# An encoder layer with Fourier and attention head groups: layout changes by transposing DMAs instead of TensorE transposes, for queries, keys and the input of the output projection

## The chip, the cores and the metric

The kernel runs on one core of a Trainium2 chip. The metric is the device time of one execution in microseconds (us). The engines are TensorE (PE: matrix products and transposes; its weight loads are listed apart as PEld), VectorE (DVE), ScalarE (ACT), GpSimd (POOL) and SyncE (SP, which here does nothing but issue DMAs). Each runs its own instructions in the order in which they were written and waits for the others through semaphores.

## The reference

One layer: RMS norm, an input projection, two head groups side by side, an output projection, a residual add and a final RMS norm. All data are float32.

```python
SEQ, N_META, D_MODEL, HEAD_DIM = 4096, 16, 1024, 64   # 8 query heads, 2 key/value heads
h = concat([meta_tokens, x])                          # 4112 tokens
u = rmsnorm(h, norm_g)
f_in, f_gate, q, k, v, a_gate = split(u @ w_in)       # widths 512, 512, 512, 128, 128, 512

# Fourier group: 8 groups of 64 channels, real part of a 2-D DFT over (tokens, channels)
fr = real(fftn(f_in.reshape(L, 8, 64), axes=(tokens, channels), norm="ortho"))
f_out = (einsum("lgc,gcd->lgd", fr, w_fmix) + b_fmix) * silu(f_gate)

# attention group
q, k = apply_rope(rmsnorm(q, q_g)), apply_rope(rmsnorm(k, k_g))
a_out = softmax(q @ k.T * 64 ** -0.5) @ v * silu(a_gate)

h = h + concat([f_out, a_out]) @ w_out
out = rmsnorm(h, final_g)[N_META:]
```

## The kernel before

**Number format.** A product of precision near float32 is made of f16 pieces: each operand is split into a high half, its f16 rounding, and a low half, the f16 rounding of the rest. The product is then hi x hi + lo x hi + hi x lo, summed in PSUM. So the tiles that feed TensorE exist as a pair of f16 tiles.

**First part, the projections** (`phase_a`). 33 token tiles of 128 tokens (the last holds the 16 meta tokens) go through the kernel one behind the other. For each tile, TensorE makes keys and values (`tile_kv`), queries (`tile_q`) and the two gates (`tile_gate`); `tile_norm` normalises and rotates queries and keys; `tile_stack` splits them into halves, with one head's high and low half side by side in 128 columns (`qs`, `ks`); and `tile_tr`, one tile later, brings them into the layout in which the attention contracts them, with the 128 columns on the partitions. It does this with four TensorE transposes for the keys (L389) and eight for the queries (L396), into PSUM tiles `kt` and `qt` of a pool with two buffers, which the small product `pr` of the row scales shares. DVE copies `kt` out and ACT copies `qt` out, and DMAs store both to DRAM (`k_d`, `q_d`, one block per tile, already transposed). A hand-made plan deals pieces of the Fourier group's fold and projection (`fold_...`, `fproj`) into four slots of each tile.

**Second part, attention and output** (`phase_b`). Keys lie in SBUF, one tile per kv head (`K0`, loaded in the first part at a point of the plan, and `K1`). Queries of a block of 512 tokens are loaded three times: as `qA` (high and low half on 128 partitions), `qB` (the high half, with rows for the score maximum below it) and `qP` (the high half of two heads above each other, for the search of the maximum). The loop runs over 32 pairs: 8 blocks of 512 tokens by 4 pairs of heads. A pair has 66 steps, 33 key tiles for each of two heads. A step makes the scores of one key tile (L1108, L1109, PSUM `s` with two buffers), an exponential on ACT (L1112), a rounding remainder on POOL or DVE (L1114), and, five steps later, the products with V (L1129 to L1136). Between the steps stand the search of the next pair's maximum (`max_units`, L1040 and the reduction L1041 on DVE) and the output projection of the block before, one 128-token tile per pair. At step 12 `out_tr` transposes the tile with eight f32 TensorE transposes (L1172), four from the mixed half `mf` and four from the attention half `obs`; ACT makes the high half `mh` and DVE the low half `ml`; the 48 products of `out_units` follow at steps 15 to 38 and 39 to 62. The last block has no following pair; its output projection is the tail, with `tail_tr` for the transposes (L1354).

**The Fourier group's end.** Its inverse (17 DFT units; `f_step`) is worked through in two stretches. Seven units stand in the initial stage, between the search groups of the first pair's maximum, and have `early` set; ten stand in the first block's attention (`block0`). A unit is: 26 or 50 products (`dft_units`, PSUM `pd`), the `gather` by three ACT instructions into `stk` (L870, L872, L873), four transposes in `trans` (L895), their split into `thl` (L897, L898 on ACT, L901 on DVE, L902 on POOL), and `mix`: products with the mixing weights (L88), the result into `mo` (on ACT, L949, and the bias on POOL, L954, for early units; on DVE, L951, for the others) and on POOL the product with the gate (L956). The rows of `mo` are then held for a DMA to `mf_d` (f32, 512 columns), which `release` issues from the SP queue when the next unit is gathered. `mo` has two buffers.

**Queues.** All loads and stores of the second part are issued by SP in the order of the program; the stores of queries and gates in the first part go through ACT's queue (`adma`).

Of the kernel before, what the change touches and what calls it, by code (L numbers as in the profile page):

```python
# [22 lines left out]
F32 = mybir.dt.float32  # L23
# [9 lines left out]
P = 128  # L33
D = 1024
# [20 lines left out]
def emit(tc, a):  # L55
# [4 lines left out]
    with top:  # L60
# [7 lines left out]
        q_d = dr.tile([NT, P, NH, P], F16, name="q_d")  # L68
        k_d = dr.tile([NT + 1, P, 4, P], F16, name="k_d")
# [3 lines left out]
        mf_d = dr.tile([NTOK, 512], F32, name="mf_d")  # L73
# [56 lines left out]
def phase_a(tc, a, pool, mm3, id16, id32, sc):  # L130
# [16 lines left out]
    with ExitStack() as st:  # L147
# [4 lines left out]
        pp = pool(st, "pp", 4, PSUM)  # L152
        pt = pool(st, "pt", 2, PSUM)
# [12 lines left out]
        ksb = [wp.tile([P, 2, 2, 2, HD], F16, name=f"ks{i}") for i in range(2)]  # L166
# [205 lines left out]
        def tile_stack(t):  # L372

            n, qn, ks = xs[t][0], live[t]["t1"], ksb[pos[t] % 2]
# [9 lines left out]
        def tile_tr(t):  # L384
            n, ks = xs.pop(t)[0], ksb[pos[t] % 2]
            z = live.pop(t)
            kt = pt.tile([P, 8, P], F16, tag="pt", name="kt")
            for i in range(4):
                T.transpose(kt[:, i, :n], ks[:n, i // 2, i % 2].rearrange("p a b->p (a b)"), id16[:n, :n])  # L389
            ko = w2.tile([P, 4, P], F16, tag="ko", name="ko")  # L390
            V.tensor_copy(ko[:, :, :n], kt[:, 0:4, :n])
            store(k_d[t, :, :, :n], ko[:, :, :n])
            if t < NT:
                qt = pt.tile([P, 8, P], F16, tag="pt", name="qt")
                for h in range(NH):
                    T.transpose(qt[:, (h % 2) * 4 + h // 2], z["qs"][:, h].rearrange("p a b->p (a b)"), id16)  # L396
# [353 lines left out]
def phase_b(tc, a, pool, mm3, id32, id16, sc):  # L750
# [6 lines left out]
    dma = nc.sync.dma_start  # L757
# [3 lines left out]
    with ExitStack() as st:  # L761
# [9 lines left out]
        K = [ld["kk"][0], bp.tile([P, NT + 1, 2, P], F16, name="K1")]  # L771
        VV = bp.tile([P, NT + 1, 2, 129], F16, name="VV")
        qA = [bp.tile([P, 4, NH, P], F16, name=f"qA{i}") for i in range(2)]
        qB = [bp.tile([P, 4, NH, P], F16, name=f"qB{i}") for i in range(2)]
        qP = [bp.tile([P, 4, 4, P], F16, name=f"qP{i}") for i in range(2)]
        nm = [bp.tile([P, P], F16, name=f"nm{i}") for i in range(2)]
        G.memset(K[1][:, NT, :, NMETA:], 0.0)
# [7 lines left out]
        def qload(b, part=(0, 1)):  # L785
            src = q_d[4 * b:4 * b + 4].rearrange("t p h c->p t h c")
            if 0 in part:
                for e in range(2):
                    dma(qP[b % 2][64 * e:64 * e + 64], src[0:64, :, 4 * e:4 * e + 4])
# [26 lines left out]
        bias, stk8 = (w2.tile([P, 512], F32, tag="mf", name=n) for n in ("bias", "stk8"))  # L816
# [117 lines left out]
        def mix(u, early):  # L934
# [21 lines left out]
            G.tensor_tensor(out=mo[:n], in0=mo[:n], in1=fgs.pop(u)[:n], op=ALU.mult)  # L956
# [605 lines left out]
```

## Time and profile before

| | us |
|---|---|
| median of three runs | 3243.61 |
| the three runs | 3244.94, 3240.65, 3243.61 |
| span of the profiled execution | 3240.9 |

| engine | busy us in the profiled execution | share of the span | instructions |
|---|---|---|---|
| PE | 3189.1 | 98% | 32919 |
| DVE | 2375.5 | 73% | 3246 |
| ACT | 1703.2 | 53% | 2969 |
| POOL | 2264.4 | 70% | 2172 |

The span reaches from the first to the last instruction of the one execution that the hardware profiler recorded; the runs are timed by themselves, and the profiled execution has its own time, 3240.9 us, just above the fastest of the three. The page gives shares of the whole span. The span consists of stages with different limits, so a share says little about any one of them; the views by stretch and the list of waits say more. In the chain of work that ended last, TensorE has 91% of the span, and the largest single rows are the scores and the products with V.

### The profile page before, as it was taken

The numbers are of one execution on the slowest core, as the hardware profiler recorded it, in microseconds if no ns is written. First come the engines' busy times: TensorE is split into PE (matmuls) and PEld (weight loads), VectorE is DVE, ScalarE is ACT, GpSimd is POOL, SyncE is SP. The second block draws the span as 40 slices with busy tenths as digits, with TensorE's granted clock in tenths as the row PEclk, the third lists the DMA queues.
The fourth block names the chain that finished last, engine by engine and source line by source line (L and its number), as shares of the span: only waits on it lengthen the run. The fifth ranks groups of instructions, "written<-read, shape, count | busy, mean of one in ns | idle before, by whom it ended". The sixth has DMA issues, their size and how long they took to land.

```text
span 3240.9 us, 78233 instructions
## 1 busy us (share of the span) xinstructions
PE 3189.1 (98%) x32919; PEld 1879.4 (58%) x32919; DVE 2375.5 (73%) x3246; ACT 1703.2 (53%) x2969; POOL 2264.4 (70%) x2172
## 2 busy tenths in 40 slices
PE   8999999998999999999999999999999999999998
PEld 4665555555666655555555555555555555555564
DVE  7656566647677777777777778777777877778764
ACT  5443433434555555555555555555555555555553
POOL 4655455536777778777777777777787777777762
PEclk9999999999999999999999999999999999999999
DMA  7443344638322210002001000100110020000011
GB/s 249 134 160 138 136 154 145 198 140 250 118 78 85 77 50 21 21 21 63 21 21 47 21 21 24 47 21 21 33 52 21 21 47 21 25 21 21 21 37 59
DMA packets 139572, 232.00 MB, mean 72 GB/s; under 512 B 22131, under 2 KB 78275, under 8 KB 136275
## 3 DMA queue, kind: packets, MB, share of 16 engines
q1 hardware_dynamic: 125394, 201.83, 19.8%
q10 hardware_dynamic: 13824, 25.17, 2.1%
q8 instruction: 257, 4.21, 0.5%
q14 instruction: 97, 0.79, 0.1%
HBM read 160.58 MB, written 66.38 MB: 70 GB/s over the span
## 4 chain that ended last, share of the span: by engine, by line
PE 91%; DVE 4%; issue 2%; DMA 1%; ACT 1%; POOL 1%; SPq 0%; ACTq 0%; POOLq 0%; DVEq 0%
PE s L1109 14%; PE s L1108 14%; PE o L1129 13%; PE po L1189 9%; PE m L1040 8%; PE o L1136 8%; PE ps L303 5%; PE ps L304 5%; PE ps L306 4%; PE o L1134 2%; PE o L1132 2%; PE pd L857 2%; PE m L1369 1%; PE m L1172 1%; PE pf L86 1%
## 5 line engine op out<-in xcount | busy, mean ns | idle before, releaser
L1114 POOL TENSOR_TENSOR rr<-pe 128x512 f16<-128x512 f32 x1572 | 1680.3, 1085 | 523.4 <-ACT pe L1112 517.9
L1112 ACT ACTIVATE pe<-s 128x512 f32<-128x512 f32 x2112 | 1260.3, 597 | 1031.8 <-PE s L1109 880.6
L1041 DVE TENSOR_REDUCE mx<-m 128x2 f32<-128x1024 f32 x1024 | 1205.7, 1219 | 174.7 <-PE m L1040 169.3
L1136 PE MATMUL o<-VV,rr 128*128 128x65 f16 x8448 | 975.9, 193 | 0.0
L1136 PEld LDWEIGHTS <-rr 128*128 128x128 f16 x8448 | 785.5, 98 | 168.8 <-POOL rr L1114 1.5
L1129 PE MATMUL o<-VV,pe 128*128 128x129 f16 x6336 | 841.0, 222 | 0.5 <-ACT tt L1140 0.4
L1109 PE MATMUL s<-qB,K 128*128 128x512 f16 x2112 | 800.6, 379 | 1.4 <-DVE qB L1076 1.4
L1129 PEld LDWEIGHTS <-pe 128*128 128x128 bf16 x6336 | 591.2, 98 | 362.1 <-issue 191.3
L1108 PE MATMUL s<-qA,K 128*128 128x512 f16 x2112 | 799.8, 379 | 0.7 <-ACT pe L1112 0.7
L1114 DVE TENSOR_TENSOR rr<-pe 128x512 f16<-128x512 f32 x540 | 450.5, 835 | 230.3 <-ACT pe L1112 225.9
L1132 PE MATMUL o<-VV,pe 128*128 128x65 f16 x2112 | 411.5, 195 | 0.0
L1134 PE MATMUL o<-VV,pe 128*128 128x64 f16 x2112 | 410.7, 194 | 0.0
L303 PE MATMUL ps<-wh,xh 128*128 128x512 f16 (+2 forms) x1032 | 353.3, 354 | 8.0 <-ACT xh L291 8.0
L304 PE MATMUL ps<-wl,xh 128*128 128x512 f16 (+2 forms) x1032 | 353.1, 354 | 2.7 <-DVE wl L274 2.7
L1040 PE MATMUL m<-K,qP 64*128 64x512 f16 x2048 | 313.2, 382 | 6.5 <-DMA qP<-q_d 2.4
L306 PE MATMUL ps<-wh,xl 128*128 128x512 f16 x768 | 292.1, 380 | 0.0
L1134 PEld LDWEIGHTS <-pe 128*128 128x128 bf16 x2112 | 209.2, 99 | 0.0
L1132 PEld LDWEIGHTS <-pe 128*128 128x128 bf16 x2112 | 206.6, 98 | 0.0
L1109 PEld LDWEIGHTS <-K 128*128 128x128 f16 x2112 | 205.2, 97 | 1.7 <-issue 1.6
L1108 PEld LDWEIGHTS <-K 128*128 128x128 f16 x2112 | 203.5, 96 | 0.9 <-issue 0.4
L1040 PEld LDWEIGHTS <-qP 64*128 64x128 f16 x2048 | 59.9, 94 | 226.5 <-issue 224.0
L1189 PE MATMUL po<-woh,mh 128*128 128x512 f16 x448 | 169.8, 379 | 0.9 <-DVE hh L1194 0.9
(213 smaller groups left out, 3561.1 us busy)
## 6 DMA issues: line engine op xcount, KB each, us to landing
room<-x SPq DMA_DIRECT2D x32, 512.0 KB
xt<-xt SPq DMA_DIRECT2D x32, 512.0 KB
sg<-fx SPq DMA_DIRECT2D x16, 1024.0 KB
xr<-x SPq DMA_DIRECT2D x32, 512.0 KB
out<-yo SPq DMA_DIRECT2D x32, 512.0 KB
ct<-cdo SPq DMA_DIRECT2D x9, 1088.0 KB
fg_d<-g ACTq DMA_DIRECT2D x32, 256.0 KB
ag_d<-g ACTq DMA_DIRECT2D x32, 256.0 KB
```

What stands on the lines that cost most here:

```text
L303: T.matmul(o, xh[:, d, :n], wh[:, d, c0:c1], start=d == 0, stop=False)
L304: T.matmul(o, xh[:, d, :n], wl[:, d, c0:c1], start=False, stop=False)
L1040: T.matmul(t[:, e], q[rs, s, p], K[kv][rs, 4 * c:4 * c + 4, 0], start=True, stop=True)
L1041: V.tensor_reduce(mx[:, s, :, c], t, axis=AX.X, op=ALU.max)
L1108: T.matmul(s, K[kv][:, t, 0], qa, start=True, stop=False)
L1109: T.matmul(s, K[kv][:, t, 1], qb, start=False, stop=True)
L1112: S.activation(pe, s, AF.Exp, scale=HD ** -0.5)
L1114: eng.tensor_tensor(out=rr, in0=pe, in1=hi, op=ALU.subtract)
L1129: T.matmul(o[:, c0:c0 + 129], hi[:, cs], va, start=t == 0 and s == 0, stop=t == NT, skip_group_check=True)
L1132: T.matmul(o[:, c0:c0 + 65], hi[:, cs], vh, start=False, stop=t == NT, skip_group_check=True)
L1134: T.matmul(o[:, c0:c0 + 64], hi[:, cs], vl, start=False, stop=t == NT, skip_group_check=True)
L1136: T.matmul(o[:, c0:c0 + 65], rr[:, cs], vh, start=False, stop=t == NT, skip_group_check=True)
```

## The change

The layout change from "tokens on the partitions" to "columns on the partitions" is done by the DMA that loads a tile, `dma_start_transpose`, at three places.

- **Queries and keys.** `tile_tr` stores `qs` and `ks` as they are, token by token; `q_d` and `k_d` become row-major. The eight and four transposes of a tile, the PSUM tiles `kt` and `qt` and their copies are gone. The PSUM pool of the transposes has one buffer instead of two (`pr` alone uses it), the projections' pool has five instead of four. `ks` has three buffers. `k_load`, `k1_load` and `qload` load with transposing DMAs; `qP` and `qB` are then copied from `qA` by DMAs from SBUF to SBUF. The layout of `K`, `qA`, `qB` and `qP` becomes head, then token.
- **The mixed half of the output projection.** `mf_d` holds two f16 halves per token (1024 columns). So `mix` splits `mo`: for each of its two versions (the unit's rows and the mirrored ones) an ACT conversion to the high half and a POOL subtraction for the low half, behind the product with the gate. The halves have two sets of buffers, `hlx` and the pair `hlmt`, `hlat`. `load_mf` becomes a transposing load into `mt`, issued at step 53 of the pair before (before: at the pair's start, untransposed).
- **The attention half.** `out_tr` splits `obs` on ACT and DVE and issues a transposing DMA from SBUF to SBUF into `at`. The eight transposes L1172 are gone.

In the tail the mixed halves of all four tiles are loaded by eight transposing DMAs at step 20 of the last pair, and `tail_tr` transposes the attention half alone on TensorE. `bias` and `stk8` lie in a tile `bs` of another buffer group.

```diff
-        q_d = dr.tile([NT, P, NH, P], F16, name="q_d")
-        k_d = dr.tile([NT + 1, P, 4, P], F16, name="k_d")
+        q_d = dr.tile([NTOK, NH * P], F16, name="q_d")
+        k_d = dr.tile([L, 4 * P], F16, name="k_d")
...
-        mf_d = dr.tile([NTOK, 512], F32, name="mf_d")
+        mf_d = dr.tile([NTOK, 1024], F16, name="mf_d")
...
-                kk.append(sh1.tile([P, NT + 1, 2, P], F16, tag="k", name="K0"))
-                nc.gpsimd.memset(kk[0][:, NT, :, NMETA:], 0.0)
+                kk.append(sh1.tile([P, 2, (NT + 1) * P], F16, tag="k", name="K0"))
+                nc.gpsimd.memset(kk[0][:, :, L:], 0.0)
             for t0, t1 in runs:
-                n = P if t1 <= NT else NMETA
-                dma(kk[0][:, t0:t1, :, :n], k_d[t0:t1, :, 0:2, :n].rearrange("t p a c->p t a c"))
+                r = slice(t0 * P, min(t1 * P, L))
+                nc.sync.dma_start_transpose(kk[0][:, :, r], k_d[r, 0:2 * P])
...
-        pp = pool(st, "pp", 4, PSUM)
-        pt = pool(st, "pt", 2, PSUM)
+        pp = pool(st, "pp", 5, PSUM)
+        pt = pool(st, "pt", 1, PSUM)
...
-        ksb = [wp.tile([P, 2, 2, 2, HD], F16, name=f"ks{i}") for i in range(2)]
+        ksb = [wp.tile([P, 2, 2, 2, HD], F16, name=f"ks{i}") for i in range(3)]
...
         def tile_tr(t):
-            n, ks = xs.pop(t)[0], ksb[pos[t] % 2]
+            n, ks = xs.pop(t)[0], ksb[pos[t] % 3]
             z = live.pop(t)
-            kt = pt.tile([P, 8, P], F16, tag="pt", name="kt")
-            for i in range(4):
-                T.transpose(kt[:, i, :n], ks[:n, i // 2, i % 2].rearrange("p a b->p (a b)"), id16[:n, :n])
-            ko = w2.tile([P, 4, P], F16, tag="ko", name="ko")
-            V.tensor_copy(ko[:, :, :n], kt[:, 0:4, :n])
-            store(k_d[t, :, :, :n], ko[:, :, :n])
+            store(k_d[t * P:t * P + n], ks[:n].rearrange("p a w b c->p (a w b c)"))
             if t < NT:
-                qt = pt.tile([P, 8, P], F16, tag="pt", name="qt")
-                for h in range(NH):
-                    T.transpose(qt[:, (h % 2) * 4 + h // 2], z["qs"][:, h].rearrange("p a b->p (a b)"), id16)
-                qo = w2.tile([P, NH, P], F16, tag="qo", name="qo")
-                S.activation(qo, qt, AF.Copy)
-                adma(q_d[t], qo)
+                adma(q_d[t * P:(t + 1) * P], z["qs"].rearrange("p h a c->p (h a c)"))
...
-    dma = nc.sync.dma_start
+    dma, dma_t = nc.sync.dma_start, nc.sync.dma_start_transpose
...
         def qload(b, part=(0, 1)):
-            src = q_d[4 * b:4 * b + 4].rearrange("t p h c->p t h c")
-            if 0 in part:
+
+            q = qA[b % 2]
+            for x in (0, 1):
+                if x in part:
+                    dma_t(q[:, 4 * x:4 * x + 4], q_d[b * QB:(b + 1) * QB, 4 * P * x:4 * P * (x + 1)])
+            for x in part:
                 for e in range(2):
-                    dma(qP[b % 2][64 * e:64 * e + 64], src[0:64, :, 4 * e:4 * e + 4])
-            if 1 in part:
-                dma(qA[b % 2], src)
-                dma(qB[b % 2][0:64], src[0:64])
+                    dma(qP[b % 2][64 * e:64 * e + 64, 2 * x:2 * x + 2], q[0:64, 4 * x + e:4 * x + 4:2])
+            for x in part:
+                dma(qB[b % 2][0:64, 4 * x:4 * x + 4], q[0:64, 4 * x:4 * x + 4])
 
         def k1_load():
-            dma(K[1][:, NT, :, :NMETA], k_d[NT, :, 2:4, :NMETA])
-            for i in range(2):
-                s = slice(16 * i, 16 * i + 16)
-                dma(K[1][:, s], k_d[s, :, 2:4].rearrange("t p a c->p t a c"))
+            for r in (slice(NT * P, L), slice(0, NTOK // 2), slice(NTOK // 2, NTOK)):
+                dma_t(K[1][:, :, r], k_d[r, 2 * P:4 * P])
...
-        bias, stk8 = (w2.tile([P, 512], F32, tag="mf", name=n) for n in ("bias", "stk8"))
+        bs = w2.tile([P, 2, 512], F32, tag="xr", name="bs")
+        bias, stk8 = bs[:, 0], bs[:, 1]
+        hlx = w2.tile([P, 2, 2, 512], F16, tag="xr", name="hlx")
+        hls = [[hlx[:, i] for i in range(2)],
+               [w1.tile([P, 2, 512], F16, tag=n, name="hl" + n) for n in ("mt", "at")]]
...
+            hl = hls[u % 2]
             for ver in range(2):
+                S.activation(hl[ver][:n, 0], mo[:n, ver], AF.Copy)
+                G.tensor_tensor(out=hl[ver][:n, 1], in0=mo[:n, ver], in1=hl[ver][:n, 0], op=ALU.subtract)
                 for p0, m, t0, st in runs_of(u, ver):
-                    held.append((rows(mf_d, t0, m, st), mo[p0:p0 + m, ver]))
+                    held.append((rows(mf_d, t0, m, st), hl[ver][p0:p0 + m].rearrange("p w c->p (w c)")))
...
-                    T.matmul(t[:, e], q[rs, s, p], K[kv][rs, 4 * c:4 * c + 4, 0], start=True, stop=True)
+                    T.matmul(t[:, e], q[rs, p, s * P:(s + 1) * P], K[kv][rs, 0, c * 512:(c + 1) * 512],
+                             start=True, stop=True)
...
         def load_mf(b, s):
-            mf = w2.tile([P, 512], F32, tag="mf", name="mf")
-            dma(mf, mf_d[b * QB + s * P:b * QB + s * P + P])
-            pst[b, s] = [mf, None]
+            mt = w1.tile([P, 8, P], F16, tag="mt", name="mt")
+            dma_t(mt, mf_d[b * QB + s * P:b * QB + s * P + P])
+            mts[b, s] = [mt]
 
         def load_xr(b, s):
-            xr = pst[b, s][-1] = w2.tile([P, D], F32, tag="xr", name="xr")
+            xr = pst[b, s] = w2.tile([P, D], F32, tag="xr", name="xr")
...
         def out_tr(b, s):
-            mf, xr = pst[b, s]
-            t = pm.tile([P, 2, 512], F32, tag="m", name="m")
-            tv = t.rearrange("p a (b c)->p (a b) c", c=P)
-            for j in range(8):
-                src = mf[:, j * P:(j + 1) * P] if j < 4 else obs[b][:, s, (j - 4) * P:(j - 3) * P]
-                T.transpose(tv[:, j], src, id32)
-            mh = ld["sh1"].tile([P, 8, P], F16, tag="mh", name="mh")
-            ml = ld["sh1"].tile([P, 8, P], F16, tag="ml", name="ml")
-            S.activation(mh, tv, AF.Copy)
-            pst[b, s] = [mh, ml, xr]
-            return lambda: V.tensor_tensor(out=ml, in0=tv, in1=mh, op=ALU.subtract)
+            src = obs[b][:, s]
+            hl = ld["sh1"].tile([P, 2, 512], F16, tag="ml" if s % 2 else "mh", name="ah")
+            S.activation(hl[:, 0], src, AF.Copy)
+
+            def low():
+                V.tensor_tensor(out=hl[:, 1], in0=src, in1=hl[:, 0], op=ALU.subtract)
+                at = w1.tile([P, 8, P], F16, tag="at", name="at")
+                dma_t(at, hl.rearrange("p w c->p (w c)"))
+                mts[b, s].append(at)
+
+            return low
...
-                T.matmul(d["po"], (ml if w == 2 else mh)[:, i],
+                T.matmul(d["po"], mts[b, s][i // 4][:, i % 4 + (4 if w == 2 else 0)],
...
+        hv, lv = (t[NQB % 2].rearrange("p h (a c)->p (h a) c", c=P) for t in (qA, qB))
...
-                out_load(b - 1, p)
+                load_xr(b - 1, p)
...
+                if i >= 4 and j == 53 and i + 1 < len(pairs):
+                    load_mf(*divmod(i - 3, 4))
...
-                    load_mf(b, 0)
-                    load_mf(b, 1)
+                    for x in range(4):
+                        t0 = b * QB + x * P
+                        dma_t(hv[:, 8 * x:8 * x + 4], mf_d[t0:t0 + P, 0:512])
+                        dma_t(lv[:, 8 * x:8 * x + 4], mf_d[t0:t0 + P, 512:1024])
...
-        tail_tr(0, 0)
-        tail_tr(1, 0)
...
-        tail_tr(0, 1)
-        tail_tr(1, 1)
-        load_mf(b, 2)
-        load_mf(b, 3)
```

Below, rows of the instruction order of single engines, before and after the change: line, operation, output and inputs, partitions by elements; `x2` counts equal neighbours. The changed kernel has its own line numbers.

The first place is ACT in the initial stage, one unit of the Fourier group between the split of its transposes (`thl`) and the gather of the next (`stk`). Before:

```order
L897 ACTIVATE thl<-s 128x512
L898 ACTIVATE thl<-thl 128x512
L949 ACTIVATE mo<-s 128x512 x2
L870 ACTIVATE stk<-pd 128x4x64
L872 ACTIVATE stk<-pd 128x4x2
L873 ACTIVATE stk<-pd 128x4x2x31
```

After:

```order
L892 ACTIVATE thl<-s 128x512
L893 ACTIVATE thl<-thl 128x512
L944 ACTIVATE mo<-s 128x512 x2
L954 ACTIVATE hlx<-mo 128x512 x2
L865 ACTIVATE stk<-pd 128x4x64
L867 ACTIVATE stk<-pd 128x4x2
L868 ACTIVATE stk<-pd 128x4x2x31
```

The two conversions L954, whose input `mo` POOL writes, now stand between the unit's own eviction and the gather of the next unit; the gather has moved behind them.

The second place is ACT in the first pair of the attention, where a unit is finished between the exponentials (`pe`). Before:

```order
L897 ACTIVATE thl<-s 128x512
L898 ACTIVATE thl<-thl 128x512
L1112 ACT_TABLE_LOAD
L1112 ACTIVATE pe<-s 128x512 x20
L870 ACTIVATE stk_7864<-pd 4x4x64
```

After:

```order
L892 ACTIVATE thl<-s 128x512
L893 ACTIVATE thl<-thl 128x512
L1111 ACT_TABLE_LOAD
L1111 ACTIVATE pe<-s 128x512 x8
L954 ACTIVATE hlmt<-mo 128x512
L954 ACTIVATE hlat<-mo 128x512
L1111 ACTIVATE pe<-s 128x512 x12
L865 ACTIVATE bs<-pd 4x4x64
```

The run of 20 exponentials is cut after the eighth by the unit's two conversions; the other twelve stand behind them.

The third place is SP's DMA queue around the second pair of a block, in which the next block's queries are loaded. Before:

```order
L1222 DMA out<-yo 128x1024
L789 DMA qP_7854<-q_d 64x4x512 x2
L791 DMA qA_7850<-q_d 128x4x1024
L792 DMA qB_7852<-q_d 64x4x1024
L1155 DMA mf<-mf_d 128x512
L1160 DMA xr<-x 128x1024
L811 DMA ag<-ag_d 128x4x128
L1222 DMA out<-yo 128x1024
```

After:

```order
L1154 DMA_TRANSPOSE mt<-mf_d 128x8x128
L780 DMA_TRANSPOSE qA_7269<-q_d 128x4x512 x2
L783 DMA qP_7273<-qA_7269 64x2x512 x4
L785 DMA qB_7271<-qA_7269 64x2048 x2
L1159 DMA xr<-x 128x1024
L802 DMA ag<-ag_d 128x4x128
L1169 DMA_TRANSPOSE at<-ah 128x8x128
L1216 DMA out<-yo 128x1024
```

The mixed half's load has moved to the end of the pair before; the queries come by two transposing loads with six copies out of `qA` behind them; and the attention half's transposing DMA stands behind all of these.

More of the change, by code (lines that the diff above doesn't have):

```diff
@@ L372, in tile_stack @@
         def tile_stack(t):
-            n, qn, ks = xs[t][0], live[t]["t1"], ksb[pos[t] % 2]
+            n, qn, ks = xs[t][0], live[t]["t1"], ksb[pos[t] % 3]
             kn = qn[:n, 8 - live[t]["o"]:]
@@ L770, in phase_b @@
         pp = pool(st, "po", 1, PSUM)
-        K = [ld["kk"][0], bp.tile([P, NT + 1, 2, P], F16, name="K1")]
+        K = [ld["kk"][0], bp.tile([P, 2, (NT + 1) * P], F16, name="K1")]
         VV = bp.tile([P, NT + 1, 2, 129], F16, name="VV")
-        qA = [bp.tile([P, 4, NH, P], F16, name=f"qA{i}") for i in range(2)]
-        qB = [bp.tile([P, 4, NH, P], F16, name=f"qB{i}") for i in range(2)]
-        qP = [bp.tile([P, 4, 4, P], F16, name=f"qP{i}") for i in range(2)]
+        qA = [bp.tile([P, NH, QB], F16, name=f"qA{i}") for i in range(2)]
+        qB = [bp.tile([P, NH, QB], F16, name=f"qB{i}") for i in range(2)]
+        qP = [bp.tile([P, 4, QB], F16, name=f"qP{i}") for i in range(2)]
         nm = [bp.tile([P, P], F16, name=f"nm{i}") for i in range(2)]
-        G.memset(K[1][:, NT, :, NMETA:], 0.0)
+        G.memset(K[1][:, :, L:], 0.0)
         G.memset(VV[:, NT], 0.0)
@@ L1053, in meta @@
                             o = 64 * x + 16 * s
[L1054 removed]
+                            T.matmul(t[:, e, o:o + 16], q[rs, x, s * P:(s + 1) * P], K[x // 2][rs, 0, NTOK:L],
                                      start=x == ps[0] and s == 0, stop=True, skip_group_check=x > ps[0] or s > 0)
@@ L1076, in put @@
                 V.tensor_tensor(
-                    out=qB[b % 2].rearrange("p s (e q) c->p e s q c", e=2)[64:72, :, :, p],
+                    out=qB[b % 2].rearrange("p (q e) (s c)->p e s q c", e=2, c=P)[64:72, :, :, p],
                     in0=t[64:72, 0, :P].unsqueeze(1).unsqueeze(1).broadcast_to([8, 2, 4, P]),
@@ L1096, in stream @@
                 h = 2 * p + e
-                qa, qb = qA[b % 2][:, :, 4 * e + p], qB[b % 2][:, :, 4 * e + p]
+                qa, qb = qA[b % 2][:, h], qB[b % 2][:, h]
                 acc = []
@@ L1107, in qk @@
                 s = pq.tile([P, 512], F32, tag="s", name="s")
-                T.matmul(s, K[kv][:, t, 0], qa, start=True, stop=False)
-                T.matmul(s, K[kv][:, t, 1], qb, start=False, stop=True)
+                T.matmul(s, K[kv][:, 0, t * P:(t + 1) * P], qa, start=True, stop=False)
+                T.matmul(s, K[kv][:, 1, t * P:(t + 1) * P], qb, start=False, stop=True)
                 pe = wk.tile([P, 512], F32, tag="pe", name="pe")
@@ L1193, in one @@
                         d["hh"] = w1.tile([P, D], F32, tag="hh", name="hh")
-                    V.scalar_tensor_tensor(out=d["hh"][:, cs], in0=d["po"], scalar=1.0 / WS, in1=xr[:, cs],
+                    V.scalar_tensor_tensor(out=d["hh"][:, cs], in0=d["po"], scalar=1.0 / WS, in1=pst[b, s][:, cs],
                                            op0=ALU.mult, op1=ALU.add)
@@ L1199, in out_end @@
         def out_end(b, s, d):
-            xr, hh = pst.pop((b, s))[-1], d["hh"]
+            xr, hh = pst.pop((b, s)), d["hh"]
             ss = sm.tile([P, 1], F32, tag="ss", name="ss")
@@ L1347, in phase_b, with tail_tr @@
         b = NQB - 1
-        hv, lv = (t[(b + 1) % 2].rearrange("p a h c->p (a h) c") for t in (qA, qB))
-        def tail_tr(s, part):
-            src = pst[b, s][0] if part == 0 else obs[b][:, s]
+        def tail_tr(s):
+            src = obs[b][:, s]
             t = pq.tile([P, 512], F32, tag="s", name="s")
@@ L1354, in tail_tr @@
                 T.transpose(t[:, j * P:(j + 1) * P], src[:, j * P:(j + 1) * P], id32)
-            x = slice(4 * (2 * s + part), 4 * (2 * s + part) + 4)
+            x = slice(8 * s + 4, 8 * s + 8)
             tv = t.rearrange("p (j c)->p j c", c=P)
@@ L1373, in tail_end @@
         def tail_end(s):
-            acc, xr = accs.pop(s), pst.pop((b, s))[1]
+            acc, xr = accs.pop(s), pst.pop((b, s))
             yo = w1.tile([P, D], F32, tag="yo" if s % 2 else "hh", name="yo")
@@ L1406, in phase_b @@
         load_xr(b, 1)
-        tail_tr(0, 1)
-        tail_tr(1, 1)
-        load_mf(b, 2)
-        load_mf(b, 3)
+        tail_tr(0)
+        tail_tr(1)
         tail_mm(0, 1)
         tail_end(0)
-        tail_tr(2, 0)
-        tail_tr(2, 1)
+        tail_tr(2)
         tail_mm(1, 1)
@@ L1418, in phase_b @@
         load_xr(b, 3)
-        tail_tr(3, 0)
-        tail_tr(3, 1)
+        tail_tr(3)
         tail_mm(2, 0)
```

7 lines of the change are left out of this document (1 added, 6 removed).

## The prediction

> **What bounds the kernel now.** I read three views in this order: busy time of each engine in stretches of the span, the chain of work that ended last, and the timeline of single engines. The rows of the first give, for each stretch, its length, then the busy us (and instructions) of PE, PE's weight loads, DVE, ACT and POOL, the granted clock, the DMA share and GB/s.
>
> ```profile
> 85.00:700.00 615.00, 610.81 (x3804) 359.22 (x3803) 374.61 (x817) 253.21 (x462) 331.59 (x236) 1.00 0.46 154
> 733.00:795.00 62.00, 50.30 (x484) 34.42 (x485) 48.46 (x47) 25.13 (x55) 41.54 (x25) 1.00 0.79 244
> 795.00:1140.00 345.00, 335.42 (x4070) 219.39 (x4070) 249.25 (x256) 182.32 (x332) 263.82 (x259) 0.99 0.32 100
> 1140.00:3100.00 1960.00, 1959.84 (x22709) 1132.43 (x22708) 1549.68 (x1787) 1116.01 (x1887) 1524.53 (x1544) 1.00 0.10 30
> ```
>
> The projection stage (85 to 700) and the main attention stage (1140 to 3100) are bound by TensorE: it is busy 99% and 100% of them at full granted clock, and the next engine, DVE, has 61% and 79%. Between them lie two stretches in which the Fourier group is finished: 733 to 795, where PE is idle 11.7 of 62 us, and 795 to 1140, where it is idle 9.6 of 345 us. So a TensorE instruction taken out saves its issue interval, and anything that makes TensorE wait costs its full length.
>
> The chain of waits says the same: in the main stage each row between other PE work is one group of eight transposes, 28 of them, one for each pair of heads.
>
> ```profile
> 1140.31 0.87 PE m L1172 x8
> 1213.71 0.87 PE m L1172 x8
> ...
> 3128.69 0.87 PE m L1172 x8
> ```
>
> **What the change takes away.** TensorE transposes, priced by their place in the issue order (start to start), since the durations overlap.
>
> ```profile
> 413.28 0.39 PE L389 MATMUL kt<-id,ks 128*128 128x128 f16 x4
> 413.50 0.61 PE L396 MATMUL qt<-id,qs 128*128 128x128 f16 x8
> 413.95 0.27 PE L86 MATMUL pf<-wcs,fh 128*128 128x248 f16 x1
> ```
>
> Main stage: 28 groups at 0.87 us are 24.4 us. Projection stage: the four key and eight query transposes of a tile stand from 413.28 to 413.95, 0.67 us; 30 of the 32 full tiles lie where PE never rests, which makes 20 us (the first two lie in the start-up, where PE waits for weights anyway, and I count nothing for them). One more wait goes with them: the small transpose of the row scales shared PSUM with the key transposes and once stood behind the copy that empties them.
>
> ```profile
> PE pr L221 <- DVE ko L391: 3.5, 1, 3.5
> ```
>
> That is 3.5 us; behind it nothing is late, since the row scales themselves were ready earlier. At the end of the kernel 16 of 32 f32 transposes go.
>
> ```profile
> 3183.29 1.05 PE s L1354 x8
> 3210.03 1.25 PE s L1354 x8
> ```
>
> Eight cost a little over 1 us, so 16 are 2.3 us; about half of them stand where ACT or DVE waits come next, so I take 1.5. The sum of the gains is 24.4 + 20 + 3.5 + 1.5 = 49 us. The evictions of PSUM by ACT and DVE go too, but those engines are not the bound, so they count as nothing.
>
> **What it adds: a wait on ACT in the Fourier mix.** The mixed tile must now be two f16 halves before it is stored. `mix` therefore gets, behind the POOL product, two ACT conversions and two POOL subtractions per unit. There are 17 units. ACT works in order, so whatever stands behind the first conversion waits until POOL has finished the product. Before, nothing on ACT followed that product. The two stretches differ in what stands behind.
>
> In the first (7 units), the next thing on ACT is the gather of the next unit's DFT (L870 to L873), which TensorE's transposes L895 need.
>
> ```profile
> 758.89 1.29 ACT L949 ACTIVATE mo<-s 128x512 f32<-128x512 f32 x2 [2.50 <-PE s L88]
> 760.86 0.38 ACT L870 ACTIVATE stk<-pd 128x256 f32<-128x256 f32 x1 [0.68 <-PE pd L854]
> 761.20 0.39 ACT L873 ACTIVATE stk<-pd 128x248 f32<-128x248 f32 x1
> 760.26 2.35 POOL L954 TENSOR_TENSOR mo<-mo,bias 128x1024 f32<-128x1024 f32 x1 [1.50 <-ACT mo L949]
> 762.69 2.35 POOL L956 TENSOR_TENSOR mo<-mo,fgu 128x1024 f32<-128x1024 f32 x1
> 761.64 0.66 PE L895 MATMUL s<-id,stk 128*128 128x128 f32 x4
> L378 ACT ACTIVATE qs<-t 128x512 f16<-128x512 f32 x32 | 19.9, 623 | 46.4 <-POOL t L363 46.4
> L954 POOL TENSOR_TENSOR mo<-mo,bias x7: 2342/2348/2356, 746.4 to 789.6; 128x1024 f32<-128x1024 f32 x7
> ```
>
> Here the gather began at 760.86, and its end at 761.59 let PE go on at 761.64 without a wait. Now it must wait for the end of the product, 762.69 + 2.35 = 765.04, and for two conversions of 128x512 f32 to f16. The nearest row is L378 with 0.62 us; two pipelined take 1.25 us. So it begins near 766.3, 5.45 us later. TensorE has nothing else to do meanwhile: the transposes stand in its fixed order, and what stands before them is the same as before. Seven units, which the last row has (789.6 - 746.4)/6 = 7.2 us apart: 38 us. DVE's reductions are late for PE in this stretch by 2.2 us in all, a wait that the longer one swallows; and POOL takes 1085 ns to subtract a tile of the size that the mix subtracts:
>
> ```profile
> PE m L1040 <- DVE mx L1041: 2.2, 3, 1.1
> L1114 POOL TENSOR_TENSOR rr<-pe 128x512 f16<-128x512 f32 x1572 | 1680.3, 1085 | 523.4 <-ACT pe L1112 517.9
> ```
>
> I take 36 us for the seven (ends: 30, if more of PE's 11.7 idle us lie in the same places; 42, if the added POOL subtractions of 1.09 us each, by the second row, come between).
>
> In the second stretch (10 units) the next thing on ACT is an exponential of the attention. The scores have two PSUM buffers, so PE can issue the scores of two more steps and then needs that exponential.
>
> ```profile
> POOL mo L956 <- DVE mo L951: 16.1, 10, 2.0
> 908.42 0.60 ACT L1112 ACTIVATE pe<-s 128x512 f32<-128x512 f32 x1 [1.91 <-PE s L1109]
> 908.73 2.35 POOL L956 TENSOR_TENSOR mo<-mo,fgu 128x1024 f32<-128x1024 f32 x1 [2.04 <-DVE mo L951]
> 907.73 0.38 PE L1108 MATMUL s<-qA,K 128*128 128x512 f16 x1
> 909.61 0.38 PE L1108 MATMUL s<-qA,K 128*128 128x512 f16 x1
> 910.71 0.38 PE L1108 MATMUL s<-qA,K 128*128 128x512 f16 x1
> ...
> 805.83 2.36 POOL L956 TENSOR_TENSOR mo<-mo,fgu 128x1024 f32<-128x1024 f32 x1 [1.82 <-DVE mo L951]
> 807.15 0.38 PE L1108 MATMUL s<-qA,K 128*128 128x512 f16 x1
> 1112.39 2.34 POOL L956 TENSOR_TENSOR mo<-mo,fgu 64x1024 f32<-64x1024 f32 x1 [1.83 <-DVE mo L951]
> 1113.84 0.38 PE L1108 MATMUL s<-qA,K 128*128 128x512 f16 x1
> ```
>
> At the unit shown first the product ends at 911.08; two conversions (1.25), the exponential that began at 908.42 before (0.60) and two hand-overs (0.1) bring it to 913.0. The third scores began at 910.71: 2.3 us of wait. The first and last of the ten units (the other rows) give 808.19 + 1.95 - 807.15 = 3.0 and 1114.73 + 1.95 - 1113.84 = 2.8. The same sum at the other seven sites gives 2.3 to 3.4; all ten make 29 us (ends 24 and 36, the second if POOL's backlog after two more subtractions reaches the products with V, five steps behind).
>
> **What it moves to the DMA queue.** Eight transposing loads fill the key tiles, 16 the query tiles, 28 the mixed tiles, 28 the attention tiles; qP and qB are now copied out of qA. No row of before shows a transposing DMA, so I bound its rate by the plain large load that stands in the chain and by a quarter of it.
>
> ```profile
> 820.42 12.79 DMA acs<-acs_d
> acs<-acs_d SPq DMA_DIRECT2D x2, 2048.0 KB
> 730.12 1.30 SPq L789 DMA_DIRECT2D qP<-q_d  x2
> 733.93 0.37 PE L1040 MATMUL m<-K,qP 64*128 64x512 f16 x1 [1.54 <-DMA qP<-q_d]
> ```
>
> 2.1 MB in 12.8 us is 164 GB/s; a quarter is 41. At the start of attention PE waited for qP, issued at 730.12 and there at 733.93. Now a transposing load of 0.5 MB comes first (3.2 us at 164, 12.8 at 41) and the copy after it, which needs no less than that hop: 3 to 13 us later. I take 4, by the nearest row. Elsewhere the cover is a count of steps: a pair of heads lasts 73.4 us (1140.31 to 1213.71) and 66 steps, 1.11 us each. The attention tile is issued at step 13 and first read at step 27, 15 us later; it is 0.26 MB, 1.6 us at 164 and 6.4 at 41. The mixed tile has 28 steps. In the second pair of a block SP must first issue the queries' two transposing loads and wait for them before six copies; that is 2.1 MB, 13 us at 164, and the attention tile behind it must be there 30 us after the pair's start. So at 164 GB/s all but the start is hidden.
>
> The Trainium skill speaks on both sides. "DMA: Bandwidth & Descriptors", section "Latency and other measured facts", gives a transposing DMA 261 GB/s effective, by which the attention tile takes an estimated 1.0 us and all of it stays hidden. "VectorE: DVE Perf Modes", section "The three transpose paths", has 390 ns for a 128x128 block on TensorE and 1309 ns by DMA; one block after another, the 32 blocks of a query load would take an estimated 42 us, and every second pair would stall. No run here shows either; the first row above shows TensorE at 0.055 us a block in a stream, so its figure is no issue interval, and the 1309 may be none either.
>
> **The sum.** -49 + 36 + 29 + 4 = +20 us. The profiled execution has a span of 3240.9 us, and its median over three runs is 3243.6 (3240.7 to 3244.9); the span lies at the low end. I add the 20 to the median: 3263 us. With all terms at their good ends (-53, 30, 24, 3) it is +4, with the bad ones (-47, 42, 36, 13) +44: 3248 to 3288.
>
> **Rivals.** *The waits are mostly covered, and it is faster.* The 17 sites average 3.8 us of wait. The change is even at (49 - 4)/17 = 2.6 us per site; below that it gains. The mechanism would be that PE arrives late at those places anyway, held by DVE. For it: PE is idle 11.7 us in the first stretch. Against it: only 2.2 us of that end with a DVE reduction, and at the transposes shown PE had no wait at all. Half the wait gives 3243.6 - 49 + 4 + 32 = 3231, none 3199. *The transposing DMA runs at a quarter of a plain load.* At 41 GB/s the queries take 25.6 us, their copies 6.4, the attention tile 6.4, hops about 4: 42 us, so PE waits 12 us in each of 7 pairs; and the second half of the keys (2.1 MB, 51 us, put in the queue at step 8 of the first pair) holds back the DFT data of 820.42 by some 34. That is +118: about 3380. It decides from about 70 GB/s down. For it: nothing measured here excludes it. Against: the DMA engines are 10% busy in the main stage, so nothing but the transposing itself could slow them. The Trainium skill's 1309 ns, block after block, would be this rival, only worse.
>
> **How the numbers follow.** The sum as it stands: 64% (3248 to 3288). Slow transposing loads: 14% (3300 to 3500). Waits half covered: 14% (3215 to 3248); hardly felt: 8% (near 3200). What a measurement of this kernel can tell from no change is about 0.2%, 6.5 us: below 3237 is faster, above 3250 slower. Faster: 8% and 8 of the half covered, 16%. Same: 6 of the half covered and 2 of the sum's low end, 8%. Slower: 62 and 14, 76%. For 8 in 10 the range takes the forecast's own, the upper part of the half covered cases and the mild end of the slow loads: 3225 to 3315.
>
> **What would show it.** In the profile after: PE's transposes L389, L396 and L1172 gone and pairs of 72.5 us instead of 73.4 (right for the gains); PE's new waits led by the stk gather and the exponentials, about 38 and 29 us, with ACT idle behind POOL's product as their source (right for the mix); the units of the first stretch near 12.5 us apart instead of 7.2; no PE wait on mt or at. Wrong would be: a wait on at, qA or K of more than a few us, pairs with queries longer than the others, or PE as busy as now in 733 to 1140.

## The result

The changed kernel takes 3272.0 us (median of four runs, 3267.6 to 3275.0) against 3243.0 us before; the ratio is 1.0091 with a 95% interval of 1.0076 to 1.0106. The profiled execution has a span of 3271.4 us, 30.5 us more than the 3240.9 of before. The forecast was 3263, in a range of 3225 to 3315.

The page of the changed kernel, busy time of the engines and the granted clock in 40 slices:

```profile
PE 3163.5 (97%) x32291; PEld 1839.8 (56%) x32291; DVE 2352.3 (72%) x3209; ACT 1671.0 (51%) x2967; POOL 2335.9 (71%) x2208
PEclk9999999997999999999999999999999999999999
```

TensorE has 628 instructions and 25.6 us of busy time less than before, and yet the kernel is longer: TensorE waits more. One slice, the tenth, has a lower clock. The busy time by stretches (columns as in the prediction), for the projections, the early Fourier units, the others and the main stage:

```profile
85.00:700.00 615.00, 612.56 (x3587) 351.84 (x3585) 377.36 (x816) 230.87 (x445) 341.12 (x241) 1.00 0.48 156
733.00:795.00 62.00, 38.92 (x283) 23.85 (x284) 27.96 (x27) 19.13 (x43) 32.63 (x23) 0.73 0.48 139
795.00:1140.00 345.00, 308.25 (x3574) 202.43 (x3572) 219.70 (x225) 171.94 (x317) 253.32 (x244) 0.96 0.31 88
1140.00:3100.00 1960.00, 1953.20 (x22744) 1118.85 (x22742) 1555.68 (x1799) 1113.03 (x1910) 1569.09 (x1562) 1.00 0.14 36
```

In 733 to 795 TensorE is idle 23.1 of 62 us (11.7 before) at a granted clock of 0.73, and in 795 to 1140 it is idle 36.8 us (9.6 before). The list of its waits says for what (in total, times, longest):

```profile
PE s L890 <- ACT stk L868: 31.7, 6, 6.9
PE s L1107 <- ACT pe L1111: 22.6, 12, 2.9
PE ps L303 <- ACT xh L291: 9.2, 2, 7.7
PE pd L852 <- ACT stk L868: 6.2, 1, 6.2
PE m L1038 <- DMA qP<-qA: 6.0, 1, 6.0
PE o L1128 <- ACT tt L1139: 3.4, 2, 3.0
```

The gather `stk` and the exponentials `pe`, both on ACT, lead it; `mt` and `at`, the tiles that come by transposing DMAs in the main stage, do not stand in it at all.

To say where the 30.5 us come from, I cut both executions at instructions that both have, by the last or first start in the groups by line: the last projection product, the first search group, the first scores, the last transposes of a Fourier unit, and the last product that turns the maximum. First before, then after:

```profile
L308 PE MATMUL ps<-wh,xl x264: 272/273/421, 11.4 to 712.4; 128*128 128x256 f16 x128, 128*16 128x256 f16 x4
L1040 PE MATMUL m<-K,qP x2048: 372/386/631, 733.9 to 3110.5; 64*128 64x512 f16 x187
L1108 PE MATMUL s<-qA,K x2112: 376/378/618, 794.5 to 3182.3; 128*128 128x512 f16 x192
L895 PE MATMUL m<-id,stk x36: 222/272/329, 864.1 to 1105.6; 128*128 128x128 f32 x32, 64*128 64x64 f32 x4
L1071 PE MATMUL m<-id,nm x32: 219/219/286, 794.4 to 3115.7; 128*128 128x128 f16 x32
```

```profile
L308 PE MATMUL ps<-wh,xl x264: 272/273/418, 11.1 to 691.7; 128*128 128x256 f16 x128, 128*16 128x256 f16 x4
L1038 PE MATMUL m<-K,qP x2048: 372/386/632, 716.4 to 3144.7; 64*128 64x512 f16 x187
L1107 PE MATMUL s<-qA,K x2112: 376/378/618, 821.3 to 3215.8; 128*128 128x512 f16 x192
L890 PE MATMUL m<-id,bs x4: 222/224/272, 1162.3 to 1162.6; 64*128 64x64 f32 x4
L1070 PE MATMUL m<-id,nm x32: 219/219/311, 821.3 to 3149.8; 128*128 128x128 f16 x32
```

The differences, with the terms of the prediction beside them (us):

| stage, up to | before | after | difference | predicted |
|---|---|---|---|---|
| projections (last L308) | 712.4 | 691.7 | -20.7 | -23.5 |
| hand-over (first search group) | 21.5 | 24.7 | +3.2 | +4 |
| initial stage (first scores) | 60.6 | 104.9 | +44.3 | +36 |
| Fourier units in the first block | 311.1 | 341.3 | +30.2 | +29 |
| main stage | 2010.1 | 1987.2 | -22.9 | -24.4 |
| tail | 125.2 | 121.6 | -3.6 | -1.5 |
| span | 3240.9 | 3271.4 | +30.5 | +20 |

The largest miss is in the initial stage. Two of the stages between the same cuts, the initial one and the one behind it (columns as above), before:

```profile
733.90:794.50 60.60, 49.92 (x483) 34.30 (x484) 47.97 (x47) 24.86 (x55) 40.64 (x24) 1.00 0.79 242
794.50:1105.60 311.10, 305.11 (x3694) 201.17 (x3694) 222.38 (x230) 165.86 (x304) 239.46 (x235) 1.00 0.31 96
```

After:

```profile
716.40:821.30 104.90, 64.12 (x483) 40.51 (x484) 48.54 (x46) 31.33 (x66) 53.56 (x37) 0.75 0.52 150
821.30:1162.60 341.30, 313.79 (x3696) 205.47 (x3693) 223.31 (x229) 174.34 (x322) 256.98 (x252) 0.97 0.29 83
```

In the initial stage TensorE has as many instructions as before, but is busy 64.1 us with them instead of 49.9, and it is idle 40.8 us instead of 10.7. So of the 44.3 us lost, 30.1 are waiting and 14.2 are slower work, at a granted clock of 0.75. In the stage behind it 21.5 are waiting and 8.7 slower work. The prediction had 36 and 29 us of waiting, and no slower work. One early unit in the timeline of the changed kernel (start, duration; in brackets idle time before and its releaser):

```profile
758.05 2.34 POOL L951 TENSOR_TENSOR mo<-mo,fgu 128x1024 f32<-128x1024 f32 x1
760.42 1.15 ACT L954 ACTIVATE hlx<-mo 128x512 f16<-128x512 f32 x2 [4.87 <-POOL mo L951]
761.48 0.36 ACT L865 ACTIVATE stk<-pd 128x256 f32<-128x256 f32 x1
762.23 1.12 PE L890 MATMUL s<-id,stk 128*128 128x128 f32 x4 [5.24 <-ACT stk L868]
766.58 0.22 PE L86 MATMUL s<-wvh,thl 128*128 128x128 f16 x1
```

POOL's product ends at 760.39, ACT converts, gathers, and TensorE has stood 5.24 us; that is the wait that was worked out (5.45). What was not worked out comes behind it: the four transposes take 1.12 us instead of 0.66, and from their start to the mixing products L86 it is 766.58 - 762.23 = 4.35 us. Before, the same instructions took 764.27 - 761.64 = 2.63 us, and the transposes started at once:

```profile
764.27 0.22 PE L86 MATMUL s<-wvh,thl 128*128 128x128 f16 x1
```

### The profile page after: what moved, and what is told of

The parts are those of the page before. It is cut to its first block, busy times and chain, and to the rows that moved or that the text cites. A ratio compares the mean times of both kernels' runs of the same rounds, so it can differ in the third digit from the quotient of the medians.

```text
span 3271.4 us, 77066 instructions
## 1 busy us (share of the span) xinstructions
PE 3163.5 (97%) x32291; PEld 1839.8 (56%) x32291; DVE 2352.3 (72%) x3209; ACT 1671.0 (51%) x2967; POOL 2335.9 (71%) x2208
## 4 chain that ended last, share of the span: by engine, by line
PE 70%; POOL 3%; DMA 1%; issue 1%; ACT 1%; DVE 1%; SPq 0%; POOLq 0%; ACTq 0%; DVEq 0%
PE s L1107 13%; PE s L1108 13%; PE o L1128 12%; PE po L1183 9%; PE m L1038 8%; PE o L1135 8%; PE o L1133 2%; PE o L1131 2%; PE pd L852 2%; PE m L1366 1%; POOL rr L1113 1%; POOL mo L951 1%; ACT pe L1111 0%; POOL mo L949 0%; DMA acs<-acs_d 0%
## 5 line engine op out<-in xcount | busy, mean ns | idle before, releaser
L1113 POOL TENSOR_TENSOR rr<-pe 128x512 f16<-128x512 f32 x1572 | 1703.5, 1101 | 477.3 <-ACT pe L1111 470.9
L1107 PE MATMUL s<-qA,K 128*128 128x512 f16 x2112 | 801.0, 379 | 22.6 <-ACT pe L1111 22.6
L1108 PEld LDWEIGHTS <-K 128*128 128x128 f16 x2112 | 205.3, 97 | 24.4 <-issue 24.3
L1183 PE MATMUL po<-woh,mt 128*128 128x512 f16 x448 | 169.8, 379 | 1.0 <-DVE hh L1188 1.0
```

The source lines that it names most:

```text
L1107: T.matmul(s, K[kv][:, 0, t * P:(t + 1) * P], qa, start=True, stop=False)
L1108: T.matmul(s, K[kv][:, 1, t * P:(t + 1) * P], qb, start=False, stop=True)
L1113: eng.tensor_tensor(out=rr, in0=pe, in1=hi, op=ALU.subtract)
L1183: T.matmul(d["po"], mts[b, s][i // 4][:, i % 4 + (4 if w == 2 else 0)], wol[i // 4][:, i % 4, cs] if w == 1 else woh[0][:, i, cs], start=j ...
```

## The experiments

Every kernel was compared with the kernel before on the same chip. Theory 1 is the prediction's: ACT stands in front of the conversions until POOL has the product, and what stands behind them on ACT is late for TensorE. Theory 2 adds that TensorE runs slower after such a wait. Rival A: the transposing loads and copies slow the two stretches. Rival B: POOL's added work is the cost.

**Later conversions.** The two conversions and subtractions of a unit are put in a list and issued later: by `mix` ahead of the next unit's evictions (the first `while`), or by `block0`, which counts down once per step (the last lines). Lines are left out at the marks:

```diff
+            while splits:
+                splits.pop(0)[1]()
...
+            def split():
+                for ver in range(2):
+                    S.activation(hl[ver][:n, 0], mo[:n, ver], AF.Copy)
...
+            splits.append([0 if early else 5, split])
...
+            for z in splits:
+                z[0] -= 1
+            while splits and splits[0][0] <= 0:
+                splits.pop(0)[1]()
```

> The conversions of a mixed unit and their subtractions are issued later: in the initial stage just ahead of the next unit's evictions, in the first block five steps later. Nothing is left out. Theory 1 (order on ACT): the stretch of the seven early units lost 44 us and that of the ten others 30 us, because ACT stood in front of the conversions until POOL's product was done; with other work in between both go, and 3272 becomes about 3200 (3192 to 3212), some 40 below the kernel before. Rival A (the transposing loads of keys and queries and the copies behind them slow these stretches): order changes nothing, 3262 to 3275. Rival B (POOL, with 2.3 us more per unit, becomes the bound of the early units: 2.35 + 2.35 + 0.61 + 2.27 = 7.6 us against 7.2 before, and its backlog holds back the products with V): 3212 to 3230.

Measured: 3207.8 us, ratio 0.989 (0.9875 to 0.9904). The two parts of it alone, with the other units as in the changed kernel:

> Only the conversions of the seven early units are issued later. Theory 1: the wait for the gather (38 us in the changed kernel) and the slow TensorE behind it go: about 3228 (3222 to 3236), the granted clock of the initial stage near 1.0 instead of 0.73, units about 7.5 us apart. Rival A (loads): 3262 to 3275. Rival C (the slow clock is not a consequence of the waits): the waits go but the clock stays near 0.73, about 3240.

Measured: 3236.0 us, ratio 0.9978 (0.9967 to 0.9989), at the upper end of what was expected. The granted clock is 0.95 in the initial stage: 0.50 and 0.52 in its first 6 us, behind a wait of 6.0 us for `qP`, and 1.00 after them.

> Only the conversions of the ten units in the first block are issued later, by five steps. Theory 1: the waits of the scores for the exponentials (20 us between 825 and 1165) go, and the 30 us that this stretch lost shrink to under 8: about 3245 (3240 to 3252). Rival B (POOL's 2.3 us more per unit are the cost, wherever they stand): 3255 to 3272.

Measured: 3247.7 us, ratio 1.0018 (1.0009 to 1.0027). The windows of the initial stage of the early part alone and of the other units of the second part alone:

```profile
714.00:776.00 62.00, 52.12 (x481) 35.13 (x482) 46.55 (x46) 28.71 (x63) 48.62 (x36) 0.95 0.80 217
```

```profile
819.00:1132.00 313.00, 305.23 (x3693) 200.90 (x3690) 227.12 (x229) 174.15 (x321) 262.61 (x251) 1.00 0.30 87
```

By the same cuts as above the initial stage falls from 104.9 to 61.8 us and the other units from 341.3 to 313.4; before, they were 60.6 and 311.1. So the place of the split explains nearly all of the loss in both. The early part alone leaves the other units 5.5 us longer than in the changed kernel (346.8); 3.0 of them are a longer wait for the DFT's data `acs`. These kernels move POOL's subtractions along with ACT's conversions; that it is ACT through which the place costs is read from the waits: with both moved, TensorE waits 0.8 us for the gather and 1.2 us for exponentials, instead of 37.9 and 22.6. POOL's and the transposing loads' work was the same here as in the changed kernel, so rivals A and B can hold only what is left: a few us, and the POOL share of it shows as 1.8 us of waits of the products with V for `rr`. The version with both is faster than either kernel of the case, by 34 us than the one before.

**Two halves of the change.**

> Only the queries' and keys' part of the change: no TensorE transposes in the projection stage, transposing loads, copies of qP and qB; mixed tiles and output projection as before. By the stages of the runs so far the projections end 21 to 24 us earlier and the first search group stands 3 us later behind them; nothing else moves: about 3223 (3219 to 3227). If loads of keys and queries were a cost in the two stretches of the Fourier units (rival A), they would be slower here too: 3230 or more.

Measured: 3227.5 us, ratio 0.9947 (0.9932 to 0.9961): faster, but 4 us short. The projections end at 688.3, as expected, but the initial stage takes 66.3 us instead of 60.6. The timeline of SP's queue and ACT in that kernel shows why:

```profile
732.13 4.03 SPq L780 DMA_TRANSPOSE qA<-q_d  x1
739.69 1.28 SPq L783 DMA_DIRECT2D qP<-qA  x2
741.01 0.61 SPq L785 DMA_DIRECT2D qB<-qA  x1
741.73 1.55 SPq L873 DMA_DIRECT2D mf_d<-mo  x2
...
749.22 1.24 ACT L940 ACTIVATE mo<-s 128x512 f32<-128x512 f32 x2 [7.47 <-DMA mf_d<-mo]
```

SP must wait for the second transposing load to land before it can issue the copies (739.69), and the store of a finished unit stands behind them. The unit after next needs that `mo` buffer: its eviction on ACT waits 7.47 us for the store, the gather behind it is late too, and TensorE waits 3.4 us. So there is a little of rival A, through the queue's order.

> Only the output projection's part: mixed tiles in f16 halves and transposing DMAs for the mixed and attention halves; queries and keys as before. If the parts add up: the stretch of the early units +44, that of the others +30, main stage -23, tail -4, sum +47: about 3289 (3283 to 3296). If the loss of the early units needs the transposing loads of keys and queries beside it, it is smaller here: 3255 to 3275.

Measured: 3291.6 us, ratio 1.0142 (1.0127 to 1.0157), with an initial stage of 105.6, 337.4 for the other units, 1987.1 for the main stage: the loss in the two stretches needs nothing of the queries' and keys' part. The two halves add up to within 4 us: -15.7 + 48.4 = +32.7 us by the medians of their own comparison, against the +29 measured for the whole.

**The slower TensorE.** Products whose results are overwritten fill the wait ahead of the transposes:

```diff
+            for _ in range(22 if early else 0):
+                T.matmul(ps.rearrange("p g c->p (g c)"), wvh[:, 0, 0], wvh[:, 1].rearrange("p g c->p (g c)"),
+                         start=True, stop=True)
             for g in range(4):
                 T.transpose(ps[:, g, :n], sk[:n, g], id32[:n, :n])
```

> The changed kernel with 22 more products of 128x128 by 128x512, whose results are overwritten, on TensorE ahead of the transposes of each early unit, where it waits about 5.2 us for the gather; at 0.216 us each they are 4.8 us and fit into the wait. Theory 2 (TensorE runs at half clock for some 4 us after a wait of 5 us, and the 1.7 us per unit by which transposes and DFT products then take longer are why the stretch lost 44 and not 36 us): the clock stays near 1.0, the transposes of four take 0.66 instead of 1.11 us, units come about 12.3 us apart instead of 13.5, and the time falls by 6 to 12 us, to 3260 to 3266. Rival (the slow stretch comes from something else, such as the transposing loads beside it): no change or a few us more, 3272 to 3280.

Measured: 3271.1 us, ratio 1.0088 (1.0073 to 1.0103), no difference from the changed kernel and not the 3260 to 3266 of theory 2. In the timeline the units of the middle did come closer, 12.4 to 13.4 us apart where the changed kernel has 13.2 to 14.5, but at the first and the last unit the products stood where TensorE does not wait for the gather, and took 6.3 and 6.4 us:

```profile
717.49 6.25 PE L890 MATMUL s<-wvh 128*128 128x512 f16 x22
...
749.01 0.66 PE L893 MATMUL s<-id,stk 128*128 128x128 f32 x4 [0.51 <-ACT stk L868]
...
761.49 0.65 PE L893 MATMUL s<-id,stk 128*128 128x128 f32 x4 [0.51 <-ACT stk L868]
...
812.79 6.39 PE L890 MATMUL s<-wvh 128*128 128x512 f16 x22
```

So the run told nothing by its time. It was repeated without those two, with `if early and 0 < u < 7`.

> As fill, but without the 22 products at the first and the last early unit: there no wait stands ahead of the transposes, and the 22 products cost 6.3 and 6.4 us by themselves, which hid the effect. Theory 2 (half clock after a wait of 5 us): units in the middle stay at 12.5 us instead of 13.8, the initial stage takes 104.9 - 6 x 1.3 = about 97 us, the time is 3264 (3259 to 3267). Rival (the slow clock costs nothing that another engine would not cost anyway): 3269 to 3275.

Measured: 3266.0 us, ratio 1.0073 (1.0056 to 1.0089). The total alone does not tell it from the changed kernel, since the intervals overlap; the stage does: 98.7 us instead of 104.9 (the two other kernels that leave the early units as they are in the changed one have 105.1 and 105.6). The stage as a whole, and two windows of its middle, which have the full clock with TensorE busy:

```profile
714.80:813.50 98.70, 82.57 (x616) 48.92 (x617) 48.44 (x46) 31.55 (x66) 53.80 (x38) 0.93 0.56 160
745.00:760.00 15.00, 13.13 (x99) 7.41 (x97) 5.31 (x5) 5.95 (x15) 9.84 (x7) 1.00 0.66 193
760.00:775.00 15.00, 13.28 (x104) 7.82 (x100) 8.99 (x9) 4.82 (x11) 7.58 (x5) 1.00 0.36 105
```

The same two windows of the changed kernel:

```profile
745.00:760.00 15.00, 8.28 (x62) 5.17 (x62) 5.32 (x5) 4.17 (x9) 8.67 (x6) 0.75 0.59 169
760.00:775.00 15.00, 8.74 (x66) 5.35 (x66) 7.58 (x7) 5.59 (x14) 8.66 (x7) 0.73 0.29 83
```

A kernel that does more on TensorE, and nothing less anywhere, is 6.2 us shorter in this stage, and its four transposes take 0.66 us. From the transposes to L86 the same products as in the unit above take 2.55 us (758.73 to 761.28), where they took 4.35 in the changed kernel and 2.63 before. The 6 times 22 added products are 28.5 of the 82.6 us of busy time at 0.216 us each; the other 54.1 us do what takes 64.1 in the changed kernel. So 10.0 us of slower work are gone, and 3.8 of them came back as waits. Theory 2 holds for the slower work; in the length of the stage it is worth 6.2 us.

**Conversions on POOL.** `S.activation(hl[ver][:n, 0], mo[:n, ver], AF.Copy)` becomes `G.tensor_copy(hl[ver][:n, 0], mo[:n, ver])`, in the same place.

> The changed kernel with the two conversions of a unit on POOL instead of ACT, in the same place of the program. ACT no longer waits for the product. Theory 1: no wait of TensorE for the gather, the initial stage is bound by POOL instead, 2.35 + 2.35 + 0.61 + 4.6 = 9.9 us per unit and about 80 us in all (62 before, 105 now); in the first block POOL does 7 us in a row per unit, and the products with V wait some 15 us in all for its backlog: about 3241 (3222 to 3255). Rival B (POOL's added work, not ACT's order, is what costs): no better than 3272, since POOL has more to do.

Measured: 3242.4 us, ratio 0.9997 (0.9987 to 1.0006), the number that was expected, but not by the sum that was expected. A conversion takes POOL 0.61 us, not 1.15, so POOL has 8.8 us of work per unit; the units are about 10.9 us apart all the same, since a small copy of the next unit (`thl`, L897) stands on POOL behind the split, and TensorE's mixing products wait for it:

```profile
L954 POOL CAST hlx<-mo x16: 609/609/1072, 731.2 to 1123.0; 128x512 f16<-128x512 f32 x16
...
PE o L1135 <- POOL rr L1113: 17.2, 13, 2.2
PE s L88 <- POOL thl L897: 15.8, 6, 4.6
```

The initial stage takes 83.7 us and the other units 333.4. POOL does 1.2 us more per unit than in the changed kernel, and the kernel is 30 us faster: against rival B. But the same illness is there in another place: what stands behind the split on the splitting engine is late.

## Why the prediction was right or wrong

**What bounds the kernel, and the sign: right.** In the two stretches between the TensorE-bound stages the added waits cost more than the transposes gave, and the main source was the order on ACT behind POOL's product, as the separate runs show. The nearness of the number is in part luck: in these two stretches the waiting was 51.6 us where 65 were forecast, and 22.9 us of slower work on TensorE, which the prediction did not have, came on top.

**Transposes of the main stage, 24.4 us: right.** 22.9 measured. By the issues of `at` (28 of them, from 1197.6 to 3166.0) a pair lasts 72.9 us, where 72.5 had been forecast.

**Projections, 23.5 us: 20.7 in the profiled execution.** In the seven other kernels with this part the projections end at 688.3 to 690.3, where before had 712.4 and the kernel without it 710.6, so the 20 us for the transposes are there. The 3.5 us for the wait behind `ko` do not show in the profiled execution: "behind it nothing is late" did not hold there. That wait is gone, but the wait for `xh` grew from 8.0 to 9.2, that of `pr` for the row scales from 2.8 to 3.4 and that of L86 for `lt` from 0.7 to 2.4: 3.5 us in all. In most of the other kernels `xh` stays near 8, so how much of the term is there in general is not shown.

**Start of attention, 4 us: right in size** (3.2). The first transposing load of 0.5 MB landed 5.4 us after its issue, where the prediction had 3.2 by the plain load's rate and 12.8 by a quarter of it:

```profile
708.34 5.43 DMA qA<-q_d
713.78 2.50 DMA qP<-qA
```

**Early units, 36 us: the mechanism was right, the sum too small.** The waits for the gather are 31.7 + 6.2 = 37.9 us, against 0.8 before, as the prediction's 38. Other waits of the stage fell from 9.5 to 2.8 us, more than the 2 us that it took off for them. The step that failed is the one that ends in "apart: 38 us": it counts the wait and then lets TensorE go on at its old pace. It does not: at the unit shown 4.35 instead of 2.63 us follow, 1.7 us more, and seven times that is an estimated 12 us. The rest of the 14.2 us of slower work stands at the start of the stage, behind the wait of 6.0 us for `qP`: from the first search group to the first L86 it is 723.05 - 716.42 = 6.6 us without a wait, where before it was 5.8 with 1.4 us of waits. The filled kernel shows that this pace hangs on TensorE's idleness and not on the data, though only 6.2 us of it came out in the length of the stage. The Trainium skill has this rule, in "TensorE: Matmul & The Clock Gate", section "HAM oscillation — how this bites in real kernels": a gap of more than some 3.4 us drops the array to half clock, and the penalty is paid again at each gap. For the early units the trace agrees, with waits of 3.8 to 6.9 us, a granted clock of 0.75 and transposes at a median of 421 instead of 273 ns; the rule would have given the missing term. But 3.4 us is no sharp limit in this trace: after a wait of 2.90 us that ended at 913.56 the clock was down too, and after one of 2.89 us that ended at 1017.10 it stayed at 1.00. What decides between the two no run here shows. The window behind the first of them (columns as above, clock 0.52):

```profile
913.50:920.00 6.50, 6.44 (x38) 3.32 (x38) 2.54 (x3) 2.33 (x6) 6.34 (x10) 0.52 0.06 17
```

**The other units, 29 us: near in size by luck.** The stretch lost 30.2 us. Of the waits for exponentials 19.9 us lie between 825 and 1165, ten of them (2.0 each, where 2.3 to 3.4 were worked out). A wait of 3.0 for `tt` also stood behind the conversions on ACT, and a weight load waited 3.2 for POOL's subtraction. In all TensorE is idle 21.5 us longer, and 8.7 us are slower work, at a mean clock of 0.97. One site in the chain:

```profile
909.50 2.35 POOL mo L951
912.41 0.61 ACT hlat L954
913.56 0.59 PE s L1107
```

**Rival "waits mostly covered": fell.** The seven waits of the early stretch are 37.9/7 = 5.4 us each, where 5.45 had been worked out; the ten others are shorter than worked out, but not covered.

**Rival "slow transposing DMA": fell.** No pair waits for `mt` or `at`. That "all but the start is hidden" is nearly right; the run with queries and keys alone shows 5.7 us more in the initial stage, by SP's order. In the changed kernel it cannot be told from the larger waits. The Trainium skill's 1309 ns per block ("VectorE: DVE Perf Modes", section "The three transpose paths") is not a rate: the 16 blocks of that first load would have taken 21 us one after another, and took 5.4. From issue to landing that is 97 GB/s for 0.5 MB, well below the 261 GB/s that the prediction quotes.

**Tail, 1.5 us: 3.6 measured**, more than the 2.3 us of the transposes themselves; what the rest is, no run here tells.

## What to carry to other kernels

When a step gets one more stage on another engine (here POOL's product, then a conversion on ACT), look at what stands behind that stage on its engine: an in-order engine turns a free dependency into a wait for everybody behind it, and moving the same instructions a few places down won 64 us of 3272 here. And where a wait leaves TensorE idle for 5 us, price the wait and then the slower time behind it: here 30.1 us of waiting in the initial stage came with 14.2 us of slower work.

## What the runs showed of the hardware that was not expected

SP is busy far longer to issue a transposing DMA than a plain one: 1.24 us for 0.26 MB, 2.26 us for 0.5 MB, where the plain stores of the output, 0.5 MB each, take 0.34; the number of DMA packets rose from 139,572 to 234,222. Rows of the groups by line of the changed kernel (min/median/max in ns):

```profile
L1154 SPq DMA_TRANSPOSE mt<-mf_d x28: 1237/1238/1767, 1175.5 to 3135.3; - x28
L780 SPq DMA_TRANSPOSE qA<-q_d x16: 1932/2258/6258, 708.3 to 2701.3; - x16
```

In this kernel SP does nothing else, so that it only matters through the order of its queue.
